# Encoder trunk on one core: first tokens loaded before adaLN, adaLN's weights as the stationary operand, and a new order of the first products

## The chip, the cores and the metric

The kernel runs on one core of one Trainium2 chip. The metric is the device time of one execution in microseconds (us); lower is better. The core has five engines that work side by side, each in its own program order: TensorE (PE; its weight loads are listed as PEld), VectorE (DVE), ScalarE (ACT), GpSimd (POOL) and SyncE (SP), which issues the DMA transfers. Engines wait for each other through semaphores.

## The reference

One layer of a bidirectional encoder over two sequences (1024 and 256 tokens, 1280 in all, of 1024 channels), in fp32. Cut to what matters here:

```python
mod = c @ w_ada + b_ada                      # c: one row for each sequence
shift, scale, gate = jnp.split(mod[:, None, :], 3, axis=-1)
h = rms_norm(x, norm_g) * (1.0 + scale) + shift
p = h @ w_in                                 # 1024 -> 11280 columns
cb, cc, cx, cz, q, k, v, o, mz, gpre, gmerge = split_combined(p)
...                                          # short convolution; chunkwise mLSTM in two directions
g_conv, g_mlstm = jnp.split(jax.nn.sigmoid(gmerge), 2, axis=-1)
merged = g_conv * (y_conv @ w_proj_conv) + g_mlstm * (y_m @ w_proj_mlstm)
return x + gate * (merged @ w_out)
```

A final RMSNorm follows. "adaLN" is the first line: shift and scale are the first 2048 columns of w_ada (8 MB), needed before anything can be multiplied with w_in. The gate third is made later in the kernel.

## The kernel before

**The big product.** h @ w_in is done by Strassen's scheme over two halves of the channels (0 to 511, "lows"; 512 to 1023, "highs") and two halves of the tokens (0 to 639 and 640 to 1279). The normalised, modulated tokens, turned so that channels lie on partitions, are four blocks of four tiles of 128 x 640 each: B11 (lows, first tokens), B21 (highs, first tokens), B12 (lows, last tokens) and B22 (highs, last tokens). From them come the operands that PE streams: b11, b21 and b22, which are the blocks themselves, and t1 to t4, which are sums and differences made on DVE by `combine`. Each operand is stored in two parts (`both_parts`): a high part, which ACT copies to the rounded type fp32r, and a low part, which DVE gets by subtraction. Weights are split in the same way by `split_op` (ACT copy, POOL subtraction). A job is one pair of 128 columns against one operand: four steps over the channel tiles, each of six matmuls of 128 x 320 (high times high, high times low, low times high, for two quarters of the tokens), so 24 matmuls for one job, accumulated in one of three PSUM buffers ("acc").

**The list of jobs.** `todo` holds the jobs in order and `go(k)` issues job k, with its weights prepared a few jobs ahead. Jobs 0 to 11 are six "corners": the products of b11 and b21 with the columns of gmerge for channel tiles n = 0, 2, 4, ..., 10. They need the first tokens alone. From job 12 on come the other five jobs of each pair (`Strassen.jobs`: t2, t3, t1, t4, b22). A corner's first product (`e_11`) is copied out by ACT and kept, in half of a "big" buffer for n = 0 to 6, or in a "q" buffer with a copy stored to DRAM for n = 8 and 10; its second (`e_12`) is added to it by DVE.

**The order.** `Board` is a planner at build time: each operation has an engine, an estimated duration in us, the tokens it reads and writes, and a step (`board.step`). The planner plays all of them with these durations and a DMA rate (`KB_US`), takes at each point the operation that can start soonest and among those nearly as soon the one with the lowest step, and so fixes the order on every engine, SP among them. On the chip each engine then goes through its list in that order.

**The beginning.** `beginning()` does what the change touches. It loads w_ada in eight pieces of 128 rows by 2048 columns (`load_wa`, two loads of 512 KB each) into the tiles that later hold the operands' parts (b00H, b00L, ..., t2L), then the token tiles (`load_x`, ten of 512 KB) and the raw weights of the first corners (`corner_load`, 512 KB each, in runs of 128 columns). PE multiplies with c as the stationary operand (128 rows by 4 columns, two of them zeros) and w_ada as the moving one, 512 columns at a time, so that the sums of all 2048 columns are complete after the last piece (L480). Four copies take the sums out of PSUM (L492), PE turns them so that channels lie on partitions (L496), and DVE adds the bias and forms scale and shift (L503 to L506).

Tokens are handled in four groups (0 to 2, 3 and 4, 5 to 7, 8 and 9). `norm_x` squares and sums them (ACT L418, DVE L414), takes the root (ACT) with a Newton step (DVE), and scales the rows (DVE L436). `turn_x` transposes a group for one channel tile on PE (L449) into one of two PSUM buffers ("misc"), and ACT (L454) or DVE (L457) writes it out with scale and shift applied. Then come `both_parts` (ACT L383, DVE L384), `combine` (DVE L389) and the jobs' matmuls (L755). L672 is the DVE addition that takes a job's sum out of PSUM, L628 a weight combination on DVE, L329 and L330 the two halves of `split_op`.

**Where things lie.** SBUF is handed out from two sides. The small tile "rows", which receives c, the biases and norm_g at the start (eight small loads on ACT's queue, then a PE transpose L253), is given back before the operand pools are made; b00 and b10 (pool hp) are on the same, right side, t2 and t3 (pool sp) on the left.

Of the kernel before, what the change touches and what calls it, by code (L numbers as in the profile page):

```python
# [9 lines left out]
F32 = mybir.dt.float32  # L10
F32R = mybir.dt.float32r
AF = mybir.ActivationFunctionType
# [169 lines left out]
def encoder_kernel(  # L182
# [150 lines left out]
    raw_a, early = {}, {}  # L333

    def corner_split(n, j):
        raw = raw_a[n]
        return split_op(lambda: raw[:].rearrange("p a (b c) -> p (a b) c", b=2)[:, 4 * j:4 * j + 4, :], [raw])

    def corner_load(n):

        raw_a[n] = raw = raw_tile()
        load(512, lambda: raw[:].rearrange("p a (b c) -> p (a b) c", b=2), win[:, :, CGM + n * P:CGM + (n + 1) * P], (), [raw])
# [49 lines left out]
    def beginning():  # L392
        junk = big()

        def cz4():
            return junk[:, D:D + 32].rearrange("p (k s) -> p k s", s=4)

        def modT():
            return junk[:, D + 32:D + 64].rearrange("p (h k s) -> p h k s", h=2, s=2)
# [9 lines left out]
        def norm_x(cs):  # L409
            n, s = len(cs), slice(cs[0], cs[-1] + 1)  # L410
            sq = [("ssq", c) for c in cs]
            for c in cs:
                if c % 2 and c < 8:
                    op("DVE", 1.3, lambda c=c: V.tensor_tensor_reduce(  # L414
                        out=junk2[:].rearrange("p a b -> p (a b)"), in0=x_at[c][0](), in1=x_at[c][0](), op0=ALU.mult,
                        op1=ALU.add, scale=1.0, scalar=0.0, accum_out=ssq[:, c:c + 1]), r=[x_at[c][1]], w=[junk2, ("ssq", c)])
                else:
                    op("ACT", 1.35, lambda c=c: A.activation(  # L418
                        junk[:, 0:D], x_at[c][0](), AF.Square, bias=zero[:, 0:1], scale=1.0,
                        accum_out=ssq[:, c:c + 1]), r=[x_at[c][1]], w=[(junk, "x"), ("ssq", c)])  # L420
# [18 lines left out]
        def turn_x(cs, kts):  # L439
# [3 lines left out]
            for kt in kts:  # L443
# [8 lines left out]
                sc, sh = s1[:, kt, smp:smp + 1], shf[:, kt, smp:smp + 1]  # L452
                if kt % 2 == (cs[0] == 3) or cs[0] > 3 and kt % 4 != 3:
                    op("ACT", .37 + .1 * len(cs), lambda px=px, dst=dst, d0=d0, sc=sc, sh=sh: A.activation(  # L454
                        dst[:, d0:d0 + tn], px[:, :tn], AF.Identity, bias=sh, scale=sc), r=[px, "s1"], w=[(dst, int(d0 > 0))])
                else:
                    op("DVE", .39 + .1 * len(cs), lambda px=px, dst=dst, d0=d0, sc=sc, sh=sh: V.tensor_scalar(  # L457
                        out=dst[:, d0:d0 + tn], in0=px[:, :tn], scalar1=sc, scalar2=sh, op0=ALU.mult, op1=ALU.add),
                       r=[px, "s1"], w=[(dst, int(d0 > 0))])


        board.step = -20
        cv_ = cols[:, 0:16].rearrange("p (s k) -> p k s", s=2)
        op("POOL", .15, lambda: G.memset(cz4(), 0.0), w=[(junk, "c")])
        op("DVE", .15, lambda: V.tensor_copy(cz4()[:, :, 0:2], cv_), r=[(junk, "c")], w=[(junk, "c")])
        op("ACT", 1.3, lambda: A.activation(ssq[:, 0:1], zero[:], AF.Sqrt, bias=zero[:, 0:1], scale=1.0), w=[("ssq", 0)])
        for kt in range(5):
            load_wa(kt)
        corner_load(0)
        for kt in range(5, KT):  # L470
            load_wa(kt)
        for c in range(4):
            load_x(c)
        corner_load(2)
        pada = [buf(psX, [P, 2, 512], F32, "acc", 3) for _ in range(2)]
        junk2 = buf(psX, [P, 2, 512], F32, "acc", 3)
        for kt in range(KT):
            for h, (wa, tok) in enumerate(wa_at[kt]):
                for j in range(2):
                    op("PE", .88, lambda h=h, j=j, kt=kt, wa=wa: PE.matmul(  # L480
                        pada[h][0:4, j, :], cz4()[:, kt, :], wa()[:, j * 512:(j + 1) * 512],
                        start=kt == 0, stop=kt == KT - 1), r=[(junk, "c"), tok], w=[(pada[h], j)])
        for c in range(4, NC):
            load_x(c)
        corner_load(4)
        mods = {}
        pm = misc_buf()
        for h in range(2):
            for j in range(2):
                m, f = buf(cp, [P, 4, P], F32, "comb", 5), (V.tensor_copy, A.copy)[j]  # L490
                row = (lambda m=m: m[0:4].rearrange("p a b -> p (a b)"))
                op(("DVE", "ACT")[j], .6, lambda h=h, j=j, f=f, row=row: f(row(), pada[h][0:4, j, :]), r=[(pada[h], j)], w=[m])  # L492

                def turn_mod(r0=8 * h + 4 * j, row=row):
                    for r in range(4):
                        PE.transpose(pm[:, 4 * (r0 + r):4 * (r0 + r) + 4], row()[:, r * P:(r + 1) * P], ident[0:4, 0:4])  # L496

                op("PE", .25, turn_mod, r=[m], w=[(pm, h, j)])

        def modulation():  # L500
            pmc = pm[:, 0:64].rearrange("p (h r l s) -> p h r l s", h=2, l=2, s=2)
            bias = cols[:, RSH:RSH + 16].rearrange("p (h k) -> p h k", h=2).unsqueeze(3).to_broadcast([P, 2, KT, 2])
            V.tensor_tensor(out=modT(), in0=pmc[:, :, :, 0, :], in1=bias, op=ALU.add)  # L503
            V.scalar_tensor_tensor(out=s1[:], in0=modT()[:, 1], scalar=1.0,
                                   in1=cols[:, RNG:RNG + 8].unsqueeze(2).to_broadcast([P, KT, 2]), op0=ALU.add, op1=ALU.mult)
            V.tensor_copy(shf[:], modT()[:, 0])  # L506

        op("DVE", .8, modulation, r=[(pm, h, j) for h in range(2) for j in range(2)], w=["s1", (junk, "m")])
# [4 lines left out]
        board.step = -6  # L513
        for cs in GROUPS[:2]:
            norm_x(cs)
        early.update({(n, j): corner_split(n, j) for j in range(2) for n in (0, 2)})
        for kt in lows:
            board.step = kt - 6
            for cs in GROUPS[:2]:
                turn_x(cs, [kt])  # L520
            both_parts("b11", B11, [kt])
        for kt in lows:
            board.step = kt // 2 - 2
# [3 lines left out]
        for k in range(12):  # L527
            if k in (0, 2, 4):
                corner_load(6 + k)
            if k == 2:  # L530
                board.step = 0
                for cs in GROUPS[2:]:
                    norm_x(cs)
                for kt in lows:
                    board.step = 0 + kt // 2
# [1304 lines left out]
```

## Time and profile before

| | us |
|---|---|
| median of 3 runs | 1707.49 (1703.44 to 1707.75) |
| the profiled execution | 1706.05 |
| its span, from first to last instruction | 1704.3 |
| PE busy in the span | 1657.9 |
| DVE, POOL, ACT busy | 996.0, 677.9, 579.4 |

How to read the profile. In a list of instructions, a row gives start, duration, engine, line and operation, the tiles written and read with their shapes, a count if several were merged, and in brackets how long the engine had been idle and what released it. L755 is a line of the kernel; "SPq" is the issue of a DMA on SP's queue. A table of windows gives for each stretch the busy time of each engine with its number of instructions, then PEclk, the granted clock of TensorE as a share of full speed, the busy share of the 16 DMA engines, and GB/s. The chain is the sequence of work and waits that ended last, followed back from the last instruction. Matmuls overlap, so the duration of one is longer than the distance from one to the next; the text goes by distances. An fp32 product appears as two weight loads and two matmuls; a product of the rounded type fp32r, or a transpose, as one of each.

### The profile page before, as it was taken

How to read it: one execution, taken by the hardware profiler on the slowest of the kernel's cores; microseconds unless marked ns; L12 is line 12 of the kernel's file. 1: busy time of each engine (PE TensorE's matmuls, PEld its weight loads, DVE VectorE, ACT ScalarE, POOL GpSimd, SP SyncE). 2: the span in 40 equal slices, each digit the busy share in tenths (PEclk: the TensorE clock that was granted, in tenths of full speed). 3: DMA queues.
4: the chain of work that ended last, by engine and by line, in shares of the span. 5: the costliest groups of instructions: out<-in, count | busy, mean ns of one | idle time of the engine just before them, and what ended most of it. 6: DMA issues, size and time to landing. Idle time of an engine off the chain costs nothing.

```text
span 1704.3 us, 27694 instructions
## 1 busy us (share of the span) xinstructions
PE 1657.9 (97%) x10542; PEld 1571.2 (92%) x10542; DVE 996.0 (58%) x1689; ACT 579.4 (34%) x1121; POOL 677.9 (40%) x499
## 2 busy tenths in 40 slices
PE   7889999999999999999999999999999999999997
PEld 1789999899999999999999999999988889898985
DVE  1795434456555655666666886652257777565645
ACT  2753232123544222222222222122256565333322
POOL 1124333234655576676667643333210101223412
PEclk9899999999999999999999999999999999999999
DMA  8224325323554122212222565558778855783631
GB/s 331 93 92 142 120 92 137 61 83 103 151 151 126 53 69 81 81 57 65 66 69 69 146 143 132 130 126 266 264 249 278 270 181 162 230 283 121 236 109 62
DMA packets 280536, 241.87 MB, mean 142 GB/s; under 512 B 96100, under 2 KB 237652, under 8 KB 280404
## 3 DMA queue, kind: packets, MB, share of 16 engines
q1 hardware_dynamic: 280224, 240.06, 46.1%
q8 instruction: 84, 1.38, 0.3%
q14 instruction: 48, 0.39, 0.1%
q10 hardware_dynamic: 180, 0.04, 0.0%
HBM read 171.16 MB, written 68.89 MB: 141 GB/s over the span
## 4 chain that ended last, share of the span: by engine, by line
PE 91%; DVE 4%; issue 1%; DMA 1%; ACT 1%; ACTq 0%; SPq 0%; POOL 0%; DVEq 0%; POOLq 0%
PE acc L755 61%; PE qc L1341 3%; PE u L1359 3%; PE accd L1515 2%; PE accd L1514 2%; PE accd L1516 2%; PE accd L1727 2%; PE accd L1728 2%; PE accd L1726 2%; PE acc L1582 2%; PE acc L1581 2%; PE acc L1583 2%; PE acc L480 2%; PE misc L1402 1%; PE misc L1442 1%
## 5 line engine op out<-in xcount | busy, mean ns | idle before, releaser
L330 POOL TENSOR_TENSOR wl<-comb,wh 128x512 fp32r<-128x512 f32 x176 | 248.2, 1411 | 290.2 <-ACT wh L329 277.8
L672 DVE TENSOR_TENSOR q<-acc,q 128x640 f32<-128x640 f32 x272 | 220.8, 819 | 217.5 <-PE acc L755 215.0
L330 POOL TENSOR_TENSOR wl<-raw,wh 128x512 fp32r<-128x512 f32 x136 | 190.0, 1398 | 243.8 <-ACT wh L329 240.7
L755 PE MATMUL acc<-xt,wh 128*128 128x320 f32 x1408 | 264.3, 310 | 0.0
L755 PEld LDWEIGHTS acc<-xt,wh 128*128 128x128 f32 x1408 | 220.8, 188 | 0.4
L329 ACT CAST wh<-comb 128x512 fp32r<-128x512 f32 x176 | 108.8, 619 | 285.4 <-PE acc L755 276.9
L329 ACT CAST wh<-raw 128x512 fp32r<-128x512 f32 x136 | 84.3, 621 | 281.9 <-PE acc L755 215.3
L755 PE MATMUL acc<-xt,wl 128*128 128x320 f32 x704 | 160.6, 310 | 0.0
L1542 POOL TENSOR_TENSOR wl<-raw,wh 128x512 fp32r<-128x512 f32 x28 | 36.3, 1299 | 232.2 <-ACT wh L1541 232.2
L755 PEld LDWEIGHTS acc<-xt,wl 128*128 128x128 f32 x704 | 117.7, 188 | 0.0
L628 DVE TENSOR_TENSOR comb<-raw 128x512 f32<-128x512 f32 x88 | 72.8, 827 | 47.3 <-DMA raw<-in_w_in_dram 31.0
L822 POOL TENSOR_TENSOR big<-big,q 128x640 f32<-128x640 f32 x48 | 78.6, 1638 | 36.9 <-DVE q L672 28.5
L572 ACT ACTIVATE q<-q,zero 128x640 f32<-128x640 f32 x76 | 63.2, 831 | 85.7 <-DVE q L672 78.6
L628 DVE TENSOR_TENSOR comb<-raw,comb 128x512 f32<-128x512 f32 x44 | 45.9, 1043 | 66.0 <-POOL wl L330 66.0
L755 PE MATMUL acc<-b11H,wh 128*128 128x320 f32 x352 | 81.4, 312 | 2.8 <-ACT wh L329 2.8
L755 PE MATMUL acc<-t2L,wh 128*128 128x320 f32 x352 | 80.2, 309 | 2.1 <-DVE t2L L384 2.1
L1514 PE MATMUL accd<-y,wh 128*128 128x320 f32 x256 | 79.6, 311 | 2.7 <-DVE og L1492 1.5
L755 PE MATMUL acc<-b00H,wh 128*128 128x320 f32 x352 | 81.9, 313 | 0.0
L755 PE MATMUL acc<-b10H,wh 128*128 128x320 f32 x352 | 80.7, 310 | 0.4 <-DVE q L672 0.4
L755 PE MATMUL acc<-t2H,wh 128*128 128x320 f32 x352 | 80.6, 310 | 0.4 <-ACT t2H L383 0.4
L755 PE MATMUL acc<-b11H,wl 128*128 128x320 f32 x352 | 80.5, 309 | 0.4 <-POOL wl L330 0.4
L755 PE MATMUL acc<-b11L,wh 128*128 128x320 f32 x352 | 80.6, 310 | 0.0
(318 smaller groups left out, 4151.1 us busy)
## 6 DMA issues: line engine op xcount, KB each, us to landing
raw<-in_w_in_dram SPq DMA_DIRECT2D x96, 256.0 KB
raw<-in_w_in_dram SPq DMA_DIRECT2D x46, 512.0 KB
th<-th_dr SPq DMA_DIRECT2D x32, 320.0 KB
th_dr<-q SPq DMA_DIRECT2D x28, 320.0 KB
raw<-in_w_proj_conv_dram SPq DMA_DIRECT2D x16, 512.0 KB
k<-kn_dr SPq DMA_DIRECT2D x64, 128.0 KB
raw<-in_w_proj_mlstm_dram SPq DMA_DIRECT2D x16, 512.0 KB
raw<-in_w_out_dram SPq DMA_DIRECT2D x16, 512.0 KB
```

Source lines behind the costliest of these rows:

```text
L329: op("ACT", .63, lambda: A.copy(wh[:], src()), r=r, w=[wh])
L330: op("POOL", 1.4, lambda: G.tensor_tensor(out=wl[:], in0=src(), in1=fp(wh[:]), op=ALU.subtract), r=[*r, wh], w=[wl])
L480: op("PE", .88, lambda h=h, j=j, kt=kt, wa=wa: PE.matmul(pada[h][0:4, j, :], cz4()[:, kt, :], wa()[:, j * 512:(j + 1) * 512], start=kt == ...
L572: A.activation(out, in_, AF.Tanh, bias=zero[:, 0:1], scale=0.5)
L628: op("DVE", .9, lambda: V.tensor_tensor(out=t[:], in0=x(), in1=y(), op=o), r=[x.tok, y.tok], w=[t])
L672: op("DVE", .82, lambda: V.tensor_tensor(out=two(dst()), in0=acc[:, :, 0:TQ], in1=two(t()), op=ALU.add), r=[acc, t.tok], w=[dst.tok])
L755: PE.matmul(acc[:, q, 0:TQ], st_[:, k_, :], m_[:, q * TQ:(q + 1) * TQ], start=k_ == 0 and n == 0, stop=k_ == 3 and n == 2)
L822: op("POOL", 1.65, lambda: G.tensor_tensor(out=dst(), in0=dst(), in1=t(), op=ALU.mult), r=[dst.tok, t.tok], w=[dst.tok])
L1341: PE.matmul(pq[:, 0:HD + 2], qTs[i][:, kd, c * P:(c + 1) * P], C[:, kd, :], start=kd == 0, stop=kd == 1)
L1359: PE.matmul(pu[:, db, 0:HD + 2], k[:, db * P:(db + 1) * P], wv[:], start=True, stop=True)
L1514: PE.matmul(accs[q][:, :TQ], wh, yH, start=kt == 0, stop=False)
L1542: op("POOL", 1.36, lambda wh=wh, wl=wl, src=src: G.tensor_tensor(out=wl[:], in0=src(), in1=fp(wh[:]), op=ALU.subtract), r=[raw, wh], w=[wl])
```

## The change

Loads. The tokens of the first two groups (0 to 4) are loaded first, then w_ada. w_ada is now cut by columns: eight pieces of all 1024 rows by 256 columns, each as two loads of 512 KB (rows 0 to 511 and 512 to 1023), taken in the order shift 0 to 255, scale 0 to 255, shift 256 to 511, scale 256 to 511, and so on. Pieces 5, 6 and 7 use the tiles of pieces 2, 3 and 4. The raw weights of the corners come as one tile for two corners and one half of the channels (`early_load`, two loads of 256 KB), the first between pieces 2 and 3.

adaLN. Each piece is multiplied with the weights as the stationary operand (128 x 128 blocks) and c as the moving one (two columns), so the result lies with channels on partitions at once; the copies L492, the transposes L496 and the zero padding go. After every second piece DVE forms scale and shift of two channel tiles (`modulation(l)`), and `turn_x` waits for those two alone (token `("s1", kt // 2)`). The sums lie in two of the "acc" buffers in turn, four pieces in each.

Corners. The order is now the six products with b11 (n = 8, 10, 0, 2, 4, 6), then the six with b21 in the same order; two corners (8 and 10, 0 and 2, 4 and 6) share one raw tile. The first two are issued ahead of the second half of the loads in the list.

Combinations. B12 becomes t1 = B12 - B11 as soon as the lows of the last tokens are there; then B22 becomes t2 = B22 - t1, B11 becomes t3 = t2 - B11, and B21 becomes t4 = B21 - t2. Before, B22 became t3, B12 became t1, and B11 became t2. Both have four sets of four DVE operations.

Smaller: the squares of `norm_x` write their unused results to two "big" buffers in SBUF (before: one "big" and one PSUM buffer), scaled transposes alternate between ACT and DVE, and the planner's DMA rate for this part is 400 instead of 375 KB per us.

```diff
+    def early_load(j, n):
+        raw_a[j, n] = raw_a[j, n + 2] = raw = raw_tile()
+        for i in range(2):
+            c = CGM + (n + 2 * i) * P
+            load(256, lambda i=i: raw[:, :, i * P:(i + 1) * P], win[:, 4 * j:4 * j + 4, c:c + P], (), [(raw, i)])
...
-    quarter("b21", hp, "b10", (((2,), ()), ((3,), ())))
-    quarter("b22", hp1, "b11", (((4,), (4, 5)), ((5,), (6, 7))))
-    quarter("t2", sp, "t2", (((6,), (8,)), ((7,), (9,))))
+    quarter("b21", hp, "b10", (((2, 5), ()), ((3, 6), ())))
+    quarter("b22", hp1, "b11", (((4, 7), ()), ((), (4, 9))))
+    quarter("t2", sp, "t2", (((), (5, 6)), ((), (7, 8))))
...
-        def load_wa(kt):
-            for h, (ap, tok) in enumerate(wa_at[kt]):
-                load(512, ap, wada[:, kt, h * D:(h + 1) * D], (), [tok])
+        pieces = (0, 4, 1, 5, 2, 6, 3, 7)
+        def load_wa(i):
+            n = pieces[i]
+            for j, (ap, tok) in enumerate(wa_at[i]):
+                load(512, lambda ap=ap: ap().rearrange("p (k n) -> p k n", k=4),
+                     wada[:, 4 * j:4 * j + 4, n * 256:(n + 1) * 256], (), [tok])
...
-                        pada[h][0:4, j, :], cz4()[:, kt, :], wa()[:, j * 512:(j + 1) * 512],
-                        start=kt == 0, stop=kt == KT - 1), r=[(junk, "c"), tok], w=[(pada[h], j)])
...
+        def modulation(l):
+            ks, t = slice(2 * l, 2 * l + 2), pm[l // 2]
+            pmc = t[:, l % 2, 0:32].rearrange("p (h k s) -> p h k s", h=2, s=2)[:, :, ks]
+            wide = (lambda c: cols[:, c + 2 * l:c + 2 * l + 2].unsqueeze(2).to_broadcast([P, 2, 2]))
+            V.tensor_tensor(out=s1[:, ks], in0=pmc[:, 1], in1=wide(RSH + 8), op=ALU.add)
+            V.scalar_tensor_tensor(out=s1[:, ks], in0=s1[:, ks], scalar=1.0, in1=wide(RNG), op0=ALU.add, op1=ALU.mult)
+            V.tensor_tensor(out=shf[:, ks], in0=pmc[:, 0], in1=wide(RSH), op=ALU.add)
+        def adaln(i):
+            n, l = pieces[i], i // 2
+            if i % 4 == 0:
+                pm[l // 2] = buf(psX, [P, 2, 512], F32, "acc", 3)
+            t = pm[l // 2]
+            for b in range(2):
+                def mm(b=b, r=2 * n + b):
+                    for k in range(KT):
+                        w = wa_at[i][k // 4][0]().rearrange("p (k n) -> p k n", k=4)
+                        PE.matmul(t[:, l % 2, 2 * r:2 * r + 2], w[:, k % 4, b * P:(b + 1) * P], cv_[:, k, :],
+                                  start=k == 0, stop=k == KT - 1)
+                op("PE", 1.0, mm, r=[tok for _, tok in wa_at[i]], w=[(t, l % 2)])
+            if i % 2:
+                op("DVE", .6, lambda: modulation(l), r=[(t, l % 2)], w=[("s1", l)])
...
+        fetch(("x", 0), ("x", 1), ("w", 0), ("w", 1), ("w", 2), (0, 8), ("w", 3))
...
+        for k in range(2):
+            go(k)
+        fetch((0, 0), ("x", 2), ("x", 3), ("w", 4), ("w", 5), (0, 4), ("w", 6), ("w", 7))
...
+        board.step = 2
+        combine(B12, B12, B11)
...
                 both_parts("b22", B22)
                 combine(B22, B22, B12)
-                board.step = 10
-                combine(B12, B12, B11)
-                board.step = 4
-                combine(B11, B22, B11, ALU.add)
-                both_parts("t2", B11)
-                board.step = 5
-                both_parts("t3", B22)
-                board.step = 12
-                combine(B21, B21, B11)
+                board.step = 0
+                both_parts("t2", B22)
+                board.step = 1
+                combine(B11, B22, B11)
+                both_parts("t3", B11)
+                board.step = 13
+                combine(B21, B21, B22)
...
-    for n, j in ((0, 0), (2, 0), (0, 1), (2, 1), (4, 0), (4, 1), (6, 0), (6, 1), (8, 0), (8, 1), (10, 0), (10, 1)):
-        add(corners[n], [j])
+    for j in range(2):
+        for n in (8, 10, 0, 2, 4, 6):
+            add(corners[n], [j])
...
-    board.KB_US, board.FIRST = 375.0, 4.0
+    board.KB_US, board.FIRST = 400.0, 4.0
```

`fetch` issues the loads in the order of its arguments, each with the work that belongs to it: `("x", g)` loads and normalises token group g, `("w", i)` loads piece i and multiplies it, `(j, n)` is an early load.

More of the change, by code (lines that the diff above doesn't have):

```diff
@@ L465, in beginning @@
[L465 to L475, printed above, removed]
@@ L485, in beginning @@
[L485 to L498, printed above, removed]
@@ L508, in beginning @@
-        op("DVE", .8, modulation, r=[(pm, h, j) for h in range(2) for j in range(2)], w=["s1", (junk, "m")])
+        pm = {}
+        def modulation(l):
[5 more added lines that the diff above has]
+            V.tensor_tensor(out=shf[:, ks], in0=pmc[:, 0], in1=wide(RSH), op=ALU.add)
@@ new lines, in fetch @@
+        def fetch(*items):
+            for it in items:
+                board.step = -20
+                if it[0] == "x":
+                    for c in GROUPS[it[1]]:
+                        load_x(c)
+                    board.step = -14 if it[1] < 2 else -11
+                    norm_x(GROUPS[it[1]])
+                elif it[0] == "w":
+                    load_wa(it[1])
+                    board.step = -16
+                    adaln(it[1])
+                else:
+                    early_load(*it)
```

88 lines of the change are left out of this document (33 added, 55 removed).

## The prediction

> **What bounds the kernel now.** I read the page first: the busy times, then the shares of the chain that ended last.
>
> ```profile
> span 1704.3 us, 27694 instructions
> ...
> PE 1657.9 (97%) x10542; PEld 1571.2 (92%) x10542; DVE 996.0 (58%) x1689; ACT 579.4 (34%) x1121; POOL 677.9 (40%) x499
> ...
> PE 91%; DVE 4%; issue 1%; DMA 1%; ACT 1%; ACTq 0%; SPq 0%; POOL 0%; DVEq 0%; POOLq 0%
> ```
>
> TensorE is busy 97% of the span, so a gain must come from its missing 46 us or from matmul time itself. Where the gaps lie, a table of windows shows (busy us and instructions of PE, weight loads, DVE, ACT, POOL; granted clock; DMA share; GB/s).
>
> ```profile
> 8.90:39.30 30.40, 30.36 (x66) 5.88 (x66) 3.87 (x7) 4.71 (x9) 1.81 (x2) 1.00 1.06 390
> 39.30:52.40 13.10, 6.03 (x32) 3.85 (x33) 11.88 (x29) 9.07 (x17) 3.18 (x3) 0.59 0.81 273
> 52.40:74.40 22.00, 19.99 (x136) 19.17 (x134) 15.93 (x29) 16.17 (x28) 4.48 (x3) 0.93 0.10 28
> 74.40:111.00 36.60, 34.27 (x235) 33.26 (x233) 32.06 (x34) 23.89 (x39) 13.54 (x9) 1.00 0.36 119
> 111.00:128.62 17.62, 13.79 (x87) 12.97 (x87) 17.11 (x23) 6.72 (x10) 1.66 (x1) 0.95 0.17 52
> 128.62:308.60 179.98, 179.97 (x1220) 179.70 (x1220) 78.03 (x98) 55.36 (x82) 69.41 (x53) 0.99 0.42 121
> ```
>
> After 128.62 us PE is full for 180 us, and the change leaves that part alone. So I price one thing: when PE reaches the point now at 128.62, the first low-part matmul of job 16 (w_b22 of channels 0). What is gained by then is kept, since PE bounds what follows. The chain of waits in order of time gives the unit prices up to there.
>
> ```profile
> 5.17 3.64 DMA b00H<-in_w_ada_dram
> ...
> 8.94 30.32 PE acc L480 x64
> 39.26 1.09 PE misc L496 x16
> ...
> 75.30 0.55 PE misc L449 x5
> 75.85 0.88 PE acc L755 x6
> ...
> 128.62 179.99 PE acc L755 x1220
> ```
>
> PE starts adaLN at 8.94 and spends 30.3 us on it (32 fp32 products, 64 records). Then come 80 transposes of 0.108 (0.55 for five) = 8.6 us, and 392 product matmuls of 0.147 (0.88 for six) = 57.5 us. These 66.1 us stay the same. 128.62 - 8.94 = 119.7; less 30.3, 66.1 and 1.1 for L496 leaves **22.2 us lost** to waiting and to half clock. That is all the order of work can win.
>
> **The change part by part.**
>
> *adaLN with the weights stationary.* 8 pieces x 2 halves x 8 k = 128 fp32 products, two weight loads and two matmuls each: 256 pairs of a 128-column load and a 2-column matmul. Nearest row: L1052, an fp32 product with 128 stationary columns and a short moving side (40). The other: L496, also 128 columns but a transpose, 16 pairs in 1.09.
>
> ```profile
> 357.76 0.19 PEld L1052 LDWEIGHTS misc<-gcol,big 128*128 128x128 f32 x1
> ...
> 357.90 0.30 PEld L1052 LDWEIGHTS misc<-gcol,big 128*128 128x128 f32 x2
> ...
> 358.12 0.19 PEld L1052 LDWEIGHTS misc<-gcol,big 128*128 128x128 f32 x1
> ```
>
> Loads start at 357.76, 357.90, (358.01), 358.12: 0.11 each. I take 0.11, so 3.5 us a piece and 28.2 for all; by L496 (0.068) it would be 17.4, by the first gap (0.14) 36. The planner's 1.0 us for 16 pairs is low: they cost 1.76. So the swap itself saves 2 us, not 13. The copies L492 and transposes L496 go; four small DVE modulations come instead, behind other PE work.
>
> *Tokens first, and the start.* The first load on SP now waits for the rows tile:
>
> ```profile
> SPq L318 <- DMA rows<-in_norm_g_dram: 2.8, 1, 2.8
> ...
> SPq L318 <- PE misc L253: 0.5, 1, 0.5
> ```
>
> b00H lies where rows lay (both on the right side); t3H doesn't, so the token loads can go out at about 0.8 us. The weights follow on SP behind that same wait, with five token loads in flight to cover it. Transfer rates: 4 KB runs in a window of adaLN loads, and a lone 512 KB load of 1 KB runs, in 40 slices:
>
> ```profile
> 13.00:15.00 2.00, 2.00 (x4) 0.34 (x3) 0.00 (x0) 0.00 (x0) 0.00 (x0) 1.00 1.01 408
> ```
> ```profile
> GB/s 0 0 0 0 0 0 0 0 0 0 0 0 67 134 82 156 119 141 261 276 424 350 357 380 357 320 216 97 30 22 7 15 15 22 22 22 22 15 0 0
> ```
>
> 0.524 MB at 408 is 1.28 us; at the plateau of about 360 it is 1.45. The first load took 3.64 from issue, so 2.36 beside its transfer. Piece 0 lands at 0.8 + 2.4 + 5 x 1.28 + 2 x 1.45 = **12.4 us**; if tokens waited as weights do, 4.4 later. Later pieces land every 2.9 us, faster than PE's 3.5, so the 1 KB runs cost nothing as long as PE takes 0.11 a pair. Twelve corner loads of 256 KB replace six of 512 KB: more issues on SP, the same bytes.
>
> *First products by half of the channels.* Six products need only channels 0 to 511 and half of adaLN. They (21 us) are what PE does between pieces 4 to 7, where now it waits for all of adaLN and the tokens' chain. One PSUM buffer of three is held by the second adaLN accumulator; the two left still alternate.
>
> *T1 first.* DVE's 16 combinations remain 16, but one set moves off the crowded stretch, and T2 no longer comes behind T3:
>
> ```profile
> L389 DVE TENSOR_TENSOR xt<-xt 128x640 f32<-128x640 f32 x16 | 14.6, 954 | 0.1
> ```
> ```profile
> PE acc L755 <- ACT wh L329: 2.8, 1, 2.8
> ...
> PE acc L755 <- DVE t2L L384: 2.1, 1, 2.1
> ```
>
> The t2 wait should go (with two of 0.4 about 2.9). The wait for wh of job 16, behind DVE, may stay: 3 us, between 0 and 6.
>
> *New waits on SP.* Pieces 5, 6 and 7 go into the tiles of 2, 3 and 4, so their loads wait for PE to finish those; behind them on SP stand the other corner loads and the stores of the sums of channels 8 and 10. PE ends piece 2 near 26, 3 near 30 and 4 near 42, so 5 and 6 land long before PE is through with the first products, and 7 lands near 47 while PE still has jobs 2 to 5. I cost this at nothing; without those products it would be up to 5 us (2.4 + 2.9) for piece 7.
>
> *Costed at nothing.* The squares' scratch in SBUF, and ACT and DVE taking turns at scaling the transposes, lie under adaLN's 28 us on PE; uncovered, one square would show 1.2 us.
>
> *Half clock at the start.* The first eight matmuls of adaLN against the next eight:
>
> ```profile
> 8.94 6.29 PE L480 MATMUL acc<-b00H,big 128*4 128x512 f32 x8 [3.80 <-DMA b00H<-in_w_ada_dram]
> ...
> 15.06 3.60 PE L480 MATMUL acc<-b00L,big 128*4 128x512 f32 x8
> ```
>
> 6.29 - 3.60 = 2.7 us, which I charge again.
>
> *Waiting after modulation.* Before a product stand modulation, transpose, scaling, ACT copy and DVE subtraction, about 4 us, twice. Piece 2 covers the first, four product steps of 0.88 the second; I leave 2.5, between 0 and 8.
>
> **Sum.** 12.4 + 28.2 + 66.1 + (2.7 + 2.5 + 3.0) = 114.9 against 128.6: 13.7 us less. The profiled execution took 1706.05 (1704.3 of span and 1.75 around it), 1.4 under the median shown. 1706.05 - 13.7 = **1692**; with the bounds of the waits and of the start 1686 to 1702.
>
> **The rivals.**
>
> *Half clock through adaLN (slower).* I cut the span at the times where the clock steps (all lie a multiple of 3.413 us apart): busy PE, then granted clock.
>
> ```profile
> 38.31:41.73 3.42, 2.03 (x19) 1.00 1.02 406
> 41.73:45.14 3.41, 0.95 (x2) 0.50 1.04 416
> 48.55:51.97 3.42, 2.82 (x11) 0.50 0.18 42
> 51.97:55.38 3.41, 3.41 (x15) 0.50 0.00 0
> 109.99:113.41 3.42, 1.84 (x12) 1.00 0.02 5
> ...
> 307.96:311.38 3.42, 1.12 (x9) 1.00 0.24 72
> 311.38:314.79 3.41, 3.41 (x15) 0.50 0.55 154
> ```
>
> A window with 1.84 busy keeps the clock and one with 1.12 loses it; yet the one with 2.03 loses it too, and 1.1 of these are L496's short transposes. 48.55 to 51.97, nearly all transposes, doesn't raise it with 2.82. So such work doesn't count as busy. If a 2-column matmul doesn't either, adaLN stays at half clock. The weight loads then slow down as well:
>
> ```profile
> L755 PEld LDWEIGHTS acc<-b00L,wh 128*128 128x128 f32 x2 | 0.6, 332 | 0.0
> ...
> L755 PEld LDWEIGHTS acc<-b00L,wh 128*128 128x128 f32 x352 | 59.3, 189 | 0.0
> ```
>
> That is 332 against 189 ns, so I price a pair at 0.22, twice 0.11. The first four pieces, with only transposes between them, cost 28.2 instead of 14.1 + 2.7: +11.4. The last four have products beside them: between nothing and +14.1, and each spell leaves up to 1.7 (half a window) on the products behind, up to three times. In all +11.4 to +30.6: 1704 to 1723, likeliest 1714. It ends slower once more than some 150 of the 256 pairs run at half clock. Against it: what didn't count here were transposes, while the new matmuls are ordinary products, whose records of 0.2 us and more follow each other without a gap. [...] Whether very short ordinary products count is shown nowhere here, which is why this rival weighs much.
>
> *Weight loads at L496's rate.* At 0.068 a pair adaLN costs 17.4, and the landing of the pieces becomes the pace, which gives back some 3 us: 1684.
>
> *The change doesn't do what it says: the order stalls.* The order within each engine is laid out with 1.0 us where PE needs 1.76, so PE falls 12 us behind its plan, and DVE's reads of accumulators sit ahead of splits that PE wants next. The pattern is there now:
>
> ```profile
> 75.41 0.82 DVE L672 TENSOR_TENSOR q<-acc,big 128x640 f32<-128x640 f32 x1 [5.04 <-PE acc L755]
> ```
>
> Two such waits on the path cost 10 us: 1702. Against it: DVE has its work spread over 100 us rather than packed into 45.
>
> **How the numbers follow.** Forecast 0.45, half clock 0.36, fast loads 0.09, stalled order 0.10. I take the forecast, since ordinary products and not transposes fill adaLN. A measurement of this kernel tells about 0.3% from no change: 1702.4 to 1712.6. Faster: 0.45 + 0.09 + 0.06 of the stalled order = 0.60. Within: 0.10 of half clock and 0.03 = 0.13. Slower: 0.26 + 0.01 = 0.27. The forecast alone gives 1686 to 1702; the range for 8 in 10 reaches from 1683 into the half-clock case at 1716, leaving out some 0.04 below and 0.14 above.
>
> **What would show it.** Right: the first token load issued near 0.8, the first adaLN matmul near 12.4, 16 pairs in about 1.8 us at clock 1.00 after the first 5 us, job 16's low parts near 115. Half clock: pairs of 0.22 and a granted clock of 0.50 from 12 to 40 us. Fast loads: pieces of 2.2 us with waits for DMA between them. Stalled order: PE waiting for DVE splits that stand behind an accumulator read. The prediction is wrong altogether if the tokens' loads wait for the rows tile too, or if PE after 128.62 is no longer full.

## The result, and the profile after

The changed kernel takes 1724.7 us (median of 4 runs, 1721.37 to 1726.24) against 1707.6 for the kernel before: 1.0103 times as long, 95% interval 1.0082 to 1.0125. It is 17 us slower, where 1692 was forecast, and it lies outside the range of 1683 to 1716. The profiled execution took 1721.37. The page of the changed kernel:

```profile
span 1719.4 us, 28077 instructions
...
PE 1676.2 (97%) x10718; PEld 1617.1 (94%) x10718; DVE 990.0 (58%) x1699; ACT 575.6 (33%) x1115; POOL 685.3 (40%) x498
```

PE is busy for 18 us more than before and idle for 3 us less (43 of 46): the loss is in busy time, not in waiting. The timeline of PE in the changed kernel shows adaLN's eight pieces (L483; start, us, count of matmuls; they are counted from one here, so piece 0 of the prediction is the first):

```profile
14.37 6.96 PE L483 MATMUL acc<-cols,b00H 128*128 128x2 f32 x32 [7.20 <-DVE ssq L419]
21.19 6.97 PE L483 MATMUL acc<-cols,b00L 128*128 128x2 f32 x32
28.69 6.98 PE L483 MATMUL acc<-cols,b10H 128*128 128x2 f32 x32
37.31 6.83 PE L483 MATMUL acc<-cols,b10L 128*128 128x2 f32 x32
52.09 4.62 PE L483 MATMUL acc<-cols,b11H 128*128 128x2 f32 x32
58.85 6.82 PE L483 MATMUL acc<-cols,b10H 128*128 128x2 f32 x32
68.24 6.82 PE L483 MATMUL acc<-cols,b10L 128*128 128x2 f32 x32
77.63 4.00 PE L483 MATMUL acc<-cols,b11H 128*128 128x2 f32 x32
```

A row holds 0.14 of its last matmul's tail (21.19 - 14.37 = 6.82 for a row of 6.96). Six of the eight pieces took 6.7 to 6.8, or 0.21 for each of their 32 pairs; the fifth and the eighth ran mostly faster, right behind products; ahead of the fifth the products' rows of two matmuls had gone from 0.73 to 0.45 at 47.7 us, so the clock had risen there. Together that is 50.0 - 8 x 0.14 = 48.9 us, where 28.2 stood in the sum. Two more groups of rows say why: the weight loads of the second piece, and of the fifth and eighth together (least, median and greatest ns), then a step of the products between two pieces:

```profile
L483 PEld LDWEIGHTS acc<-cols,b11H x64: 187/192/338, 52.0 to 81.3; 128*128 128x128 f32 x64
...
L483 PEld LDWEIGHTS acc<-cols,b00L x32: 333/333/333, 21.1 to 27.7; 128*128 128x128 f32 x32
```
```profile
57.11 0.88 PE L755 MATMUL acc<-b00H,wh 128*128 128x320 f32 x2
...
58.85 1.49 PE L483 MATMUL acc<-cols,b10H 128*128 128x2 f32 x7
```

In the second piece a load took 333 ns, which is the figure of half clock in the prediction's rows (332 against 189). In the fifth and eighth, with the same two columns, the median is 192, and in the fifth, while the granted clock is 1.00, a pair takes 0.112. So a pair of two columns isn't slow in itself: it is slow where the clock is low. The six products of a step took 58.85 - 57.11 = 1.74, twice the 0.88 of before. A table of windows (PE, weight loads, DVE, ACT, POOL; granted clock; DMA share; GB/s) shows the clock itself in the later part:

```profile
14.37:21.19 6.82, 6.82 (x33) 6.82 (x33) 4.29 (x14) 0.22 (x1) 0.00 (x0) 1.00 1.10 342
50.00:55.00 5.00, 5.00 (x41) 5.00 (x39) 4.66 (x17) 1.25 (x3) 0.00 (x0) 0.95 0.03 7
...
60.00:75.00 15.00, 15.00 (x71) 15.00 (x72) 2.35 (x6) 1.84 (x3) 1.83 (x2) 0.50 0.27 85
```

From 60 to 75 us PE is busy without a gap at a granted clock of 0.50. The first row has to be read with care: its column says 1.00 while the loads inside it take 333 ns. The column reads 1.00 on both sides of 47.7 us, where the pace of the products rises, and 0.50 from 54.6 to 75, so at the head of this trace the pace counts and not the column.

The rest of the way, in the timelines of PE, POOL and DVE:

```profile
114.04 0.56 PE L755 MATMUL acc<-b10H,wh 128*128 128x320 f32 x2 [1.83 <-DVE q L671]
...
120.28 0.56 PE L755 MATMUL acc<-b10H,wh 128*128 128x320 f32 x2 [2.45 <-DVE q L671]
...
142.10 0.31 PE L755 MATMUL acc<-b11H,wl 128*128 128x320 f32 x1
```
```profile
105.79 8.60 POOL L330 TENSOR_TENSOR wl<-raw,wh 128x512 fp32r<-128x512 f32 x1 [4.99 <-ACT wh L329]
114.35 1.30 POOL L330 TENSOR_TENSOR wl<-raw,wh 128x512 fp32r<-128x512 f32 x1
```
```profile
101.41 3.02 DVE L387 TENSOR_TENSOR xt<-xt 128x640 f32<-128x640 f32 x4
...
110.23 3.02 DVE L382 TENSOR_TENSOR t3L<-xt,t3H 128x640 fp32r<-128x640 f32 x4
113.18 0.81 DVE L671 TENSOR_TENSOR q<-acc,q 128x640 f32<-128x640 f32 x1
118.07 0.69 DVE L627 TENSOR_TENSOR comb<-raw 128x512 f32<-128x512 f32 x1 [4.08 <-DMA raw<-in_w_in_dram]
```

Job 16's first low part comes at 142.10, 13.5 later than before. The waits for t2 and for wh are gone. In their place PE waits twice for a q on DVE, 4.3 us together: once because q stands behind sixteen instructions of the new order without a gap, once because q stands behind a comb that waits 4.08 for its weights. The weights came late because the tile was given free late: POOL's subtraction took 8.60 instead of 1.30. It ended at 114.39, and 1.30 before that is 113.1, just where DVE's stretch ends and q begins (113.18). So its delay fits the rest of the stretch: from 105.79 to 113.18 DVE ran about ten instructions of 0.74 (sixteen from 101.41 to 113.18), one behind the other. Why POOL was held up over ten of them is not shown.

### The profile page after: what moved, and what is told of

Same layout as the page of the kernel before. It is cut to its first block, busy times and chain, and to the rows that moved or that the text cites. A ratio compares the mean times of both kernels' runs of the same rounds, so it can differ in the third digit from the quotient of the medians.

```text
span 1719.4 us, 28077 instructions
## 1 busy us (share of the span) xinstructions
PE 1676.2 (97%) x10718; PEld 1617.1 (94%) x10718; DVE 990.0 (58%) x1699; ACT 575.6 (33%) x1115; POOL 685.3 (40%) x498
## 4 chain that ended last, share of the span: by engine, by line
PE 64%; DVE 2%; DMA 1%; ACT 1%; issue 0%; POOL 0%; SPq 0%; ACTq 0%; DVEq 0%; POOLq 0%
PE acc L755 37%; PE qc L1342 3%; PE u L1360 3%; PE accd L1515 2%; PE accd L1516 2%; PE accd L1517 2%; PE accd L1728 2%; PE accd L1729 2%; PE accd L1727 2%; PE acc L1582 2%; PE acc L1583 2%; PE acc L1584 2%; PE misc L1403 1%; PE misc L1443 1%; DMA th<-ym_dr 1%
## 5 line engine op out<-in xcount | busy, mean ns | idle before, releaser
L330 POOL TENSOR_TENSOR wl<-raw,wh 128x512 fp32r<-128x512 f32 x136 | 197.1, 1451 | 261.9 <-ACT wh L329 259.2
L1543 POOL TENSOR_TENSOR wl<-raw,wh 128x512 fp32r<-128x512 f32 x28 | 36.2, 1297 | 232.5 <-ACT wh L1542 226.2
L627 DVE TENSOR_TENSOR comb<-raw 128x512 f32<-128x512 f32 x88 | 75.3, 856 | 53.1 <-DMA raw<-in_w_in_dram 28.2
L755 PE MATMUL acc<-b00L,wh 128*128 128x320 f32 x352 | 81.8, 313 | 0.0
L755 PE MATMUL acc<-b00H,wl 128*128 128x320 f32 x352 | 81.4, 312 | 0.0
L755 PE MATMUL acc<-t3H,wh 128*128 128x320 f32 x352 | 80.2, 309 | 0.0
```

The lines of the kernel that those rows point to most:

```text
L330: op("POOL", 1.4, lambda: G.tensor_tensor(out=wl[:], in0=src(), in1=fp(wh[:]), op=ALU.subtract), r=[*r, wh], w=[wl])
L627: op("DVE", .9, lambda: V.tensor_tensor(out=t[:], in0=x(), in1=y(), op=o), r=[x.tok, y.tok], w=[t])
L755: PE.matmul(acc[:, q, 0:TQ], st_[:, k_, :], m_[:, q * TQ:(q + 1) * TQ], start=k_ == 0 and n == 0, stop=k_ == 3 and n == 2)
L1543: op("POOL", 1.36, lambda wh=wh, wl=wl, src=src: G.tensor_tensor(out=wl[:], in0=src(), in1=fp(wh[:]), op=ALU.subtract), r=[raw, wh], w=[wl])
```

## The experiments

Theory after the result: matmuls with two moving columns don't raise the clock and don't keep it up, so adaLN holds TensorE at half clock, and the products between its pieces suffer too. Its rivals: a pair costs 0.21 at any clock (the 192 ns above already speak against it); or the new waits and the new order cost the time. The first three runs change only how many columns move; the fourth changes which operand does, and with it the order. Where two of the later runs differ by 2.5 us or less, their intervals overlap; there the times tell nothing, and the text goes by the traces.

**c repeated over 128 columns** (MOVE = 128). The sums of each pair are computed 64 times over and lie further apart in PSUM; the order on every engine stays. The main line of the edit:

```diff
-                        PE.matmul(t[:, l % 2, 2 * r:2 * r + 2], w[:, k % 4, b * P:(b + 1) * P], cv_[:, k, :],
+                        PE.matmul(t[:, l % 2, 128 * r:128 * r + MOVE], w[:, k % 4, b * P:(b + 1) * P],
+                                  cv_[:, k, :].unsqueeze(1).to_broadcast([P, MOVE // 2, 2]),
```

> The changed kernel with one edit: the moving side of adaLN is c repeated over 128 columns instead of 2 (the first two columns of each sum are used); loads, order on every engine and weight loads are the same. Theory A (half clock: matmuls that stream few columns do not keep TensorE's clock up, and the 128-column weight loads slow down with it): the array now streams nearly all the time, so after the first 5 us 32 pairs take 3.5 to 4.2 us instead of 6.8, the products between the pieces run at full clock, job 16 starts near 120 us instead of 141.5, and the time is 1698 to 1706, 20 us or more under the changed kernel. Theory B (a pair of a 128-column fp32 load and a short matmul costs 0.22 by itself, whatever the clock): pieces stay at 6.8 us and the time at 1721 to 1727. Theory C (the pieces' landing or the order laid out by hand sets the pace): time within 5 us of the changed kernel, with PE waiting for DMA or DVE where it was in adaLN before.

Measured: 1696.49 (1694.96 to 1699.57), 0.9938 of before [0.9922, 0.9955]; 28 us less than the changed kernel by doing more, 24.9 of them by job 16 in the two traces (142.10 and 117.25). In the timeline of PE the first piece starts at half clock and all later ones run at full clock:

```profile
14.66 5.72 PE L484 MATMUL acc<-cols,b00H 128*128 128x128 f32 x32 [7.33 <-DVE ssq L420]
20.22 3.74 PE L484 MATMUL acc<-cols,b00L 128*128 128x128 f32 x32
...
117.25 0.45 PE L757 MATMUL acc<-b11H,wl 128*128 128x320 f32 x2
```

With 0.16 of tail in a row, 32 pairs take 3.58, so 0.112 each: the forecast's price. The loads, the order and the weight loads are the same, and the waits for q shrank by 1.5 alone (2.8 for 4.3), so both rivals fall as the cause of the 28 us. The new place of the sums isn't the cause either: the run with 16 columns below has it too.

**64 and 16 columns** (MOVE = 64, MOVE = 16).

> As wide128, with 64 moving columns. Theory A: the columns stream during about half of each pair at full clock; windows with PE busy 54% kept the clock in the kernel before, so it may hold once it is up, while raising it may fail: between 1698 and 1726, and the clock of each 3.41 us window tells which. Theory B: 1721 to 1727. Theory C: as wide128.

> As wide128, with 16 moving columns: streaming for about an eighth of each pair. Theory A: too little to count, pieces of 6.8 us as in the changed kernel, span within 3 us of its 1719.4. Theory B: the same span, so this run tells nothing between A and B; it bounds the number of columns that counts.

Measured: 64 columns 1707.31, 1.0009 of before [0.9999, 1.002]; 16 columns 1719.54 in a single run. Pieces 1, 4, 5 and 8 with 64 columns, and below them 1, 5 and 6 with 16:

```profile
14.04 7.06 PE L484 MATMUL acc<-cols,b00H 128*128 128x64 f32 x32 [6.76 <-DMA b00H<-in_w_ada_dram]
...
37.09 6.93 PE L484 MATMUL acc<-cols,b10L 128*128 128x64 f32 x32
52.32 3.68 PE L484 MATMUL acc<-cols,b11H 128*128 128x64 f32 x32
...
66.96 3.68 PE L484 MATMUL acc<-cols,b11H 128*128 128x64 f32 x32
```
```profile
14.26 6.98 PE L484 MATMUL acc<-cols,b00H 128*128 128x16 f32 x32 [6.48 <-DVE rt L427]
...
52.27 4.34 PE L484 MATMUL acc<-cols,b11H 128*128 128x16 f32 x32
58.73 6.84 PE L484 MATMUL acc<-cols,b10H 128*128 128x16 f32 x32
```

With 64 columns the first four pieces, with transposes alone between them, don't raise the clock, but once it has risen during the products between pieces 4 and 5 (their rows go from 0.73 to 0.46 near 48 us), the last four keep it, with products between them. With 16 columns a piece loses it again, as with two: the fifth starts at full pace and ends at half, and the sixth is slow throughout. (The seventh and eighth, 3.90 and 4.16, ran mostly at full pace, right behind products.) So in this kernel 128 columns raise the clock, 64 keep it with the help of the products between, 16 do neither; nothing between these numbers was tried.

**c stationary again**, 256 columns of w_ada moving, with the copy and transposes that this needs; the pieces by columns, the token loads, the corners and T1 first as changed. The planner is told 1.72 us for half a piece instead of 1.0, so the order on the engines differs.

```diff
-                        PE.matmul(t[:, l % 2, 2 * r:2 * r + 2], w[:, k % 4, b * P:(b + 1) * P], cv_[:, k, :],
+                    PE.matmul(t[0:2, l % 2, 256 * h:256 * h + 256], cv_[:, k, :], w[:, k % 4, :],
...
+                op("ACT", .58, lambda t=t: A.copy(row(), t[0:2, l % 2, :]), r=[(t, l % 2)], w=[m])
...
+                        PE.transpose(px[:, 2 * r:2 * r + 2], row()[:, r * P:(r + 1) * P], ident[0:2, 0:2])
```

> The changed kernel with one part undone: c is the stationary operand again (two columns) and the 256 columns of a piece stream; two rows of sums per piece are copied out by ACT, turned by four short transposes and then used as before. Loads by 256 columns, tokens first, corners by halves and T1 first stay; the planner gets 1.72 us per half piece, so the order on the engines differs a little. Theory A: 256 columns keep the array streaming, pieces take 3.5 us after the first 5 us, job 16 starts near 117 to 122 us, time 1698 to 1706. Theory B: the same, since no 128-column loads are left. Theory C: within 5 us of the changed kernel, 1719 to 1729.

Measured: 1704.4 (1701.22 to 1706.1), 0.9986 of before [0.9977, 0.9995]: undoing the swap, with the order that comes with it, takes back 20 us. The pieces run at full clock again (rows of 3.62 to 3.85 us a piece behind a first of 5.97), and PE waits for the copy and the scaled transposes instead. Waits of PE:

```profile
PE acc L767 <- DVE q L683: 4.0, 2, 2.5
PE misc L447 <- ACT xt L452: 1.7, 2, 1.1
PE misc L497 <- ACT comb L493: 1.6, 1, 1.6
```

The 8 us to the 1696.49 of 128 columns can't be put down to the swap, since the order differs too: the next run has the swap, the full clock and a planner told 1.8, and it took 1705.69, no less than this one. What the swap itself gains at full clock is therefore not shown. The other runs start from the kernel with 128 columns and ask what its remaining waits cost.

**The planner told 1.8 us for a half piece.**

```diff
-                op("PE", 1.0, mm, r=[tok for _, tok in wa_at[i]], w=[(t, l % 2)])
+                op("PE", 1.8, mm, r=[tok for _, tok in wa_at[i]], w=[(t, l % 2)])
```

> wide128 with one number changed: the planner is told 1.8 us instead of 1.0 for a half piece of adaLN. Theory 'the order stalls': PE's two waits for DVE's q at the end of the first products (2.8 us in wide128, 4.3 in the changed kernel) come from a plan in which PE is too early; with 1.8 they go and job 16's first low part moves from 117.25 to about 114.5, time about 1693.7. Rival: with the clock full the plan's error costs nothing that another order doesn't cost elsewhere; job 16 within 1 us of 117.25, time 1696.5 +- 1.

Measured: 1705.69, 0.9997 of before [0.9988, 1.0006], 9 us more than with 1.0; neither theory forecast that. The truer number gives an order with the first four pieces in a row, and PE then waits for the scaled transposes as well:

```profile
PE acc L757 <- DVE q L673: 4.0, 2, 2.5
PE misc L448 <- ACT xt L453: 2.4, 2, 1.7
PE misc L448 <- DVE xt L456: 1.9, 1, 1.9
```

The rival of the stalled order blamed the low estimate. It was not the cause of these waits: 4.0 us for q stay with the true one.

**The clock raised before adaLN.**

```diff
+        def warm(t=pm[0]):
+            for _ in range(22):
+                PE.matmul(t[:, 0, 0:P], ones[:], ident[:], start=True, stop=True)
+        board.step = -20
+        op("PE", 5.0, warm, w=[(pm[0], 0)])
```

> wide128 with 22 fp32 products of ones by the identity, 128 columns each, on PE while it waits for the first weights (their sums are overwritten). Theory (wide products count as activity, and the first adaLN piece runs at half clock only because PE was idle before): the first half piece takes 1.9 instead of about 3.7 us, piece 0 takes 3.74 instead of 5.72, job 16's first low part at 115.3, time about 1694.5. Rival: the clock is not raised by them, or the spell before is lost again at the wait for the tokens' weights: piece 0 still 5.7, time 1696.5.

Measured: 1694.95, 0.9932 of before [0.9916, 0.9949]. The first piece runs at full pace (rows of 1.06 for 8 pairs and 2.95 for the other 24) and is over in 4.08 us instead of 5.56, a wait of 0.23 for its weights included. The eighth piece starts at 52.30 instead of 54.66, of which 0.9 is an earlier start of adaLN, but job 16's low part comes only 0.9 earlier, at 116.36: the waits for q grew from 2.8 to 4.4.

**T1 not first.** The combinations and their steps as in the kernel before.

> wide128 with the order of the combinations (T1, T2, T3) of the kernel before put back: this undoes that part of the change alone. Theory: T1 first took away the wait of PE for t2 (2.1 us there); without it the wait comes back, job 16's first low part at about 119 to 120, time 1698.5 to 1699.5. Rival: another wait (DVE's q) ends last there anyway: job 16 within 1 us of 117.25, time 1696.5 +- 1.

Measured: 1698.89, 0.996 of before [0.9945, 0.9975], 2.4 more than with T1 first in the medians; in the traces job 16's low part comes at 120.46, 3.2 later. The waits of PE for wh and t2, as in the kernel before, are back:

```profile
PE acc L757 <- ACT wh L330: 2.8, 1, 2.8
PE acc L757 <- DVE t2L L383: 1.3, 2, 1.0
```

**Token group 1 behind the first two pieces.**

```diff
-        fetch(("x", 0), ("x", 1), ("w", 0), ("w", 1), ("w", 2), (0, 8), ("w", 3))
+        fetch(("x", 0), ("w", 0), ("w", 1), ("x", 1), ("w", 2), (0, 8), ("w", 3))
```

> wide128 with the second group of tokens fetched behind the first two pieces of the weights instead of ahead of them. Theory: two 512 KB loads less ahead of piece 0 (1.28 us each) start adaLN at about 12.1 instead of 14.66; PE is the bound from there on, so job 16's first low part comes 2.5 earlier, at 114.7, time about 1694. Rival: the tokens' chain or the landing of pieces 1 to 3 becomes late by as much: PE waits between the pieces, job 16 at 117 +- 1, time 1696.5.

Measured: 1698.98, 0.9958 of before [0.9943, 0.9973]. adaLN starts at 10.87, 3.8 earlier, yet job 16's low part comes at 118.65. The start was given back at the pieces' landing and at q:

```profile
PE acc L757 <- DVE q L673: 4.1, 2, 2.6
...
PE acc L484 <- DMA b11H<-in_w_ada_dram: 1.8, 2, 1.4
PE acc L484 <- DMA b10H<-in_w_ada_dram: 1.2, 2, 0.9
```

In both runs that bring adaLN forward, the waits for q take a part of it back, so the last runs go at q.

**Three low parts on DVE instead of POOL.**

```diff
-            return split_op(lambda: raw[:, :, i * P:(i + 1) * P], [(raw, i)])
+            return split_op(lambda: raw[:, :, i * P:(i + 1) * P], [(raw, i)], **(dict(eng=("DVE", .7, V)) if j == 1 and self.n in (2, 4, 6) else {}))
```

> wide128 with the last three subtractions for low weight parts of the corner jobs on DVE instead of POOL (PE's order unchanged). In wide128 POOL took 11.09 us for these three (1.28 to 1.59 for one alone before), all beside DVE's twelve combination instructions from 76.54 to 88.3; they free the weight tiles, and DVE's next weight combination then waited 4.10 for the load. Theory (DVE's crowded stretch slows POOL, POOL's late release makes PE's second wait for q): the three take under 1 us each on DVE right behind the stretch, at about 88.3 to 90.2; the second wait of PE for q (0.94) goes, the first grows from 1.84 to about 3.5 since q stands behind them; job 16's first low part within 1.5 us of 117.25. Rival (POOL's time isn't stretched by DVE but by its own wait for wh): on DVE they wait as long, and both PE waits grow, job 16 past 119.

Measured: 1694.59, 0.9937 of before [0.9922, 0.9952]; job 16 at 117.17. DVE's timeline:

```profile
87.77 1.89 DVE L331 TENSOR_TENSOR wl<-raw,wh 128x512 fp32r<-128x512 f32 x3
...
92.28 0.69 DVE L629 TENSOR_TENSOR comb<-raw 128x512 f32<-128x512 f32 x1 [0.43 <-DMA raw<-in_w_in_dram]
```

Three subtractions take 1.89 together, the wait for raw shrinks from 4.10 to 0.43, and PE's second wait is gone. The first is 3.73, since q stands behind them. Of the chain, low part, free tile, load, comb, q, this shows that it starts at the low parts and ends at q. Job 16 stays where it was, as forecast, and the time isn't clear of the 1696.49 of 128 columns.

**The casts earlier** (t2 due at step 4, t3 at 6), alone and with the raised clock.

> wide128 with t2's and t3's due steps 4 and 6 instead of 0 and 1: on PE, DVE, POOL and SP the order is the same, on ACT one cast of wh goes ahead of the t2H casts and one ahead of the t3H casts. Theory (the chain behind PE's waits is wh cast, low part on POOL, free weight tile, load, DVE's comb, q): POOL starts its three subtractions about 3 us earlier than 80.92 and ends them that much earlier than 92.0, DVE's wait for raw shrinks from 4.1 to about 1, PE's second wait for q (0.94) and the half clock behind the first (about 2 us) go; job 16 at about 114.5, time about 1694. Rival (the first wait for q, behind the twelve combinations, decides alone): the waits for q stay within 0.5 us and so does the time, 1696.5.

> wide128 with warm_start's 22 products ahead of adaLN and casts_early's due steps. In warm_start the 2.36 us won at the start shrank to 0.9 at job 16 (116.36 against 117.25), since the two waits for q grew from 2.8 to 4.4. Theory (those waits hang on the weight tiles that POOL frees): with the tiles free earlier the waits shrink as in casts_early and the start's gain is kept: job 16 at 112.5 to 113.5, time about 1692. Rival: the waits take the gain back again, job 16 at 115 to 116.4, time 1694.5 to 1695.

Measured: 1700.58 (0.9966 [0.9952, 0.998]) and 1698.7 (0.9957 [0.9944, 0.9969]): 4 us worse than without, against both theories. POOL did start earlier, in DVE's stretch, and DVE paid. The stretch on DVE, and POOL beside it, in the first of the two:

```profile
76.66 4.11 DVE L388 TENSOR_TENSOR xt<-xt 128x640 f32<-128x640 f32 x4
...
84.74 4.11 DVE L388 TENSOR_TENSOR xt<-xt 128x640 f32<-128x640 f32 x4
88.78 3.02 DVE L383 TENSOR_TENSOR t3L<-xt,t3H 128x640 fp32r<-128x640 f32 x4
```
```profile
77.39 1.97 POOL L331 TENSOR_TENSOR wl<-raw,wh 128x512 fp32r<-128x512 f32 x1 [1.33 <-ACT wh L330]
82.13 2.00 POOL L331 TENSOR_TENSOR wl<-raw,wh 128x512 fp32r<-128x512 f32 x1 [2.77 <-ACT wh L330]
84.43 1.53 POOL L331 TENSOR_TENSOR wl<-raw,wh 128x512 fp32r<-128x512 f32 x1 [0.29 <-ACT wh L330]
```

Each POOL subtraction adds 1.1 to the DVE group in which it falls (4.11 against 3.02). The stretch ends 3.4 later and PE's one wait for q is 5.1. The delay is on both sides: here POOL lost at most 0.7 (2.00 against 1.30), about one DVE instruction of 0.74, and DVE lost 1.1. Why POOL lost 0.7 here and 7.3 in the changed kernel's order is not shown.

**Clock raised, low parts on DVE, and q ahead of t3** (t2 due at 6, t3 at 9).

> wide128 with warm_start's 22 products, low_parts_on_dve's three subtractions on DVE, and t2's and t3's due steps 6 and 9 instead of 0 and 1, which on DVE puts the three subtractions between t2's instructions and the three q additions ahead of t3's eight instructions (PE's order unchanged). Theory (PE's remaining waits come from q standing behind DVE's crowded stretch, and POOL and DVE slow each other in it): the waits for q (4.4 us in warm_start, 3.7 in low_parts_on_dve) and the half clock behind them (about 2 us) go, at most 1.5 us of a new wait for t1's parts comes; job 16's first low part at 110.5 to 112.5, time 1689 to 1691. Rival (DVE has too much work in this stretch whatever its order): the wait comes back at t3 or t1 with 3 us or more, job 16 at 115 or later, time 1693 to 1695.

Measured: 1690.48 (1688.98 to 1693.57), 0.9908 of before [0.9894, 0.9921]; 34 us less than the changed kernel, and the fastest of all. PE's longest waits in the first 130 us for the products of jobs 0 to 16:

```profile
PE acc L765 <- ACT wh L330: 1.1, 1, 1.1
PE acc L765 <- POOL wl L331: 0.9, 1, 0.9
```

No wait for q is left. Job 16's low part comes at 113.23, 0.7 behind the expected bound, since the new 2.0 of waiting is for job 16's own weights and not for t1.

## Why the prediction was wrong

**The step that failed** is the choice of the likeliest case: "I take the forecast, since ordinary products and not transposes fill adaLN." The rows had shown transposes alone that don't count (2.82 us of 3.42 busy with them, and the clock still 0.50 behind), and I let the kind of instruction decide. The runs show that the number of moving columns decides: the same kind of product, from the same weights in the same order, doesn't raise the clock with 2 or 16 columns (rows of 6.8 to 7.0 for the first four pieces), and loses one that was raised (4.62, then 6.82 with 2), but raises and keeps it with 128 (5.72, then 3.74 to 3.85).

**The sum, term by term** (us; the last column is the kernel with 128 columns):

| term | forecast | changed kernel | 128 columns |
|---|---|---|---|
| start of adaLN | 12.4 | 14.4 | 14.7 |
| adaLN, its half-clock start included | 30.9 | 48.9 | 30.7 |
| transposes and products at full clock | 66.1 | 66.1 | 66.1 |
| waits for DVE, ACT and POOL, and half clock on transposes and products | 5.5 | 12.7 | 5.7 |
| job 16's first low part | 114.9 | 142.1 | 117.2 |

The last term but one is the remainder: 142.1 - 14.4 - 48.9 - 66.1 = 12.7, of which the waits for q are 4.3, so half clock took about 8.4. Half clock in all: 48.9 - 30.9 + 8.4 = 26.4 of the 27.2 by which job 16 is later than forecast; the start adds 2.0 and the waits, 4.3 for 5.5, take 1.2 off. Where the clock is kept, the sum holds but for the start, in part by luck: its 5.5 stood for other waits than the 5.7 that came.

**The half-clock rival** was the right one: with 2 columns the weight loads took 333 ns and a pair 0.21, and with 128 the pace was full again (0.112). Its extra of 11.4 to 30.6 holds the 26.4, and its pair of 0.22 the measured 0.21. Its time of 1714 was too low: the products behind the short pieces lost 8.4 where three spells of at most 1.7 were allowed, and the start came 2.0 late. It had 0.36, and the range ended inside its bounds at 1716; its own upper bound, 1723, lies between the profiled execution and the median.

**The forecast's own bounds.** The 1702 at their upper end is less than the terms allow: 5.5 more of waiting after modulation, 3.0 more for wh and 4.4 more at the start make 1705. This didn't decide the outcome.

**The start.** The first token load went out at 0.74, as forecast. Then SP waited, in the waits of its queue:

```profile
SPq L318 <- DMA t3H<-in_x_prompt_dram: 2.7, 1, 2.7
SPq L318 <- DMA rows<-in_b_ada_dram: 1.2, 1, 1.2
```

The third token load waited for an earlier load of t3H, and the weights went out at 7.20. I had all five token loads in flight at once. Why the third waits for the first's landing wasn't tried.

**Pairs at 0.11** was right at full clock (0.112), and L496's 0.068 was not reached. **The waits** were of the forecast size and came from another place: the t2 wait went, as said, and T1 first is worth some 3 us by job 16 in the traces; but DVE's stretch brought q. The waits on SP for the tiles of earlier pieces cost nothing, as said: PE waited for none of these loads, with 2 columns or with 128. **The stalled order** saw PE and DVE's accumulator reads in each other's way, but the other way round: here the read, q, stands behind combinations and splits, and the planner's low estimate was not the reason. Behind job 16 the changed kernel took 1719.4 - 142.1 = 1577.3 to its end, 1.6 more than before.

## What to carry to other kernels

Turning a product so that its moving side becomes a few columns can cost more than it saves: here TensorE stayed at half clock, and so did products beside it (1.74 us a step for 0.88), so look at the duration of the weight loads (333 against about 189 ns here) before the busy share. Where the operand can be repeated, moving 128 columns instead of 2 cost nothing here (0.112 a pair at full clock with either) and kept the clock. A run of sixteen DVE combinations and subtractions held up one of POOL's subtractions here (8.60 us for 1.30), and in another order such a run was held up by them (4.11 for four DVE instructions against 3.02); put what PE waits for ahead of such a run.

## What the runs showed of the hardware that was not expected

Whether adaLN's matmuls raised the clock went here by the number of moving columns: 2 and 16 did not (6.8 to 7.0 for each of the first four pieces), 128 did within the first piece (5.72, then 3.74), and 64 kept full clock over four pieces (3.68 a piece) with products between them, and couldn't raise it in four others (6.9 to 7.1 a piece) with transposes between them. Whether keeping the clock takes less than raising it, or the products made the difference, is not shown. One POOL subtraction of 1.30 lasted 8.60 beside a stretch of sixteen DVE instructions without a gap, past the end of that stretch, while in another order the same subtraction delayed DVE by 1.1 and itself took up to 2.00. And the column of the granted clock read 1.00 at the head of the changed kernel's trace (14.37 to 21.19 us) while the weight loads took 333 ns in the median.
